# Logit steps of a differential attention, issued one by one or two at a time, in a two-layer fp32 encoder on one NeuronCore

## The chip, the core and the metric

The kernel runs on one core of a Trainium2 chip. A core has a matrix engine (PE, with its weight loads shown apart as PEld), a vector engine (DVE), a scalar engine for activations and scaled copies (ACT), a general-purpose engine (POOL), and a queue (SP) from which nearly all DMAs are issued here. Operands lie in an on-chip memory of 128 partitions; matrix products are written to a small accumulation memory (PSUM) of eight banks of 128 x 512 fp32, which DVE and ACT read. The engines run side by side and wait for each other on semaphores; each works through its own queue in order.

The metric is the time of one execution on the device in microseconds (us), the median of three runs.

## What is computed

Two layers over a sequence of 512 tokens of width 1024. Layer 0 mixes tokens by differential attention, layer 1 by a gated linear attention; each layer also attends to 256 memory tokens with four heads of 64, and is followed by a gated MLP with a short convolution. All is fp32. The change lies in layer 0:

```python
# differential attention: 6 heads, two maps of width 64 each, query blocks of 128
q = rms_norm(q, g0) * 64 ** -0.5;  k = rms_norm(k, g1)
logits = einsum('bhmqd,bhmkd->bhmqk', qb, k) + bias      # block-causal mask, chunks of 64
p = softmax(logits);  w = p[:, :, 0] - lam * p[:, :, 1]
o = rms_norm(einsum('bhqk,bhkv->bhqv', w, v), g) * (1 - lam_init)

# memory attention of the same layer
kv = rms_norm(mem, g) @ w_kv;  k, v = split(kv)
o_mem = softmax(rms_norm(q_mem) * 64 ** -0.5 @ rms_norm(k).T) @ v

x = x + concat([o, o_mem]) @ w_out
h = rms_norm(x);  u = conv(h @ w_up) + b;  a, g = split(u)
x = x + (silu(g) * a) @ w_down
```

## The kernel before

**The large products.** Every matrix product with weights is made in three passes: activations and weights are each split into a rounded part and a rest (`whi`/`wlo`, `xsh`/`xsl`; lines 253 and 256 for weights, 310 and 311 for activations), and high x high, high x low and low x high are added up in a bank (lines 330 to 332 for the input projections, 351 to 353 for the others). Weights arrive in blocks of up to 128 x 1024 in a ring of three `raw` tiles, ACT casts them and DVE subtracts.

**Filler.** In layer 0 the attention is written out as a script, `SCRIPT`, which `do` reads word by word. A number is a credit in us: `F.fill` takes that much from a queue of units of the large products (six products of 512 columns count 1.3, three count 0.65). A letter with a number is a step of the attention. So the script is the order in which PE gets its work; PE's queue is the only one in which the order is written by hand. DVE, ACT, POOL and SP get the order that the scheduler of the building layer makes of the same program.

**Steps.** Three pairs of heads (0/1, 2/3, 4/5) have five steps each, numbered 0 to 14 through all pairs: each step covers one or two query blocks with 512 or 384 + 128 or 256 + 256 key columns (`TOGETHER`), so that the logits of one map fill one bank. For step t:

- `Lt` (`logits`, line 719): products of 64 rows, the two maps on the two halves of the array, into two banks of tag `lg`; then for each map a minimum with the bias on DVE (`nmd`, line 726), an exponential on ACT (line 729), and on DVE the weights `p0 - lam * p1` (lines 734 to 738).
- `Mt`: the same with banks of tag `tp`. The entry exists in the table of letters, and the script before does not use it.
- `Tt` (`turn`): four transposes of the weights into a `tp` bank, copied out by ACT (line 748).
- `Vt` (`values`, line 760): products with v into the head's `sm` bank; behind a head's last one stands its normalisation (`output`, four squares on ACT, line 771).
- `Ph` (`prepare`): head h's q and k are turned by eight transposes into two `tp` banks, copied out by ACT (line 682). `Fh` turns the head's output into operands of the output projection; `sh` scales it.

The memory attention has its own letters. `a` and `b` split the memory tokens for the keys and values of layer 0 and 1 (four calls each, two row tiles at a time; `b3` is the last for layer 1, and the units of ("kv", 1) read it). `q0` normalises the memory queries, `q1` turns them by eight transposes through `tp` (line 582 copies out). `k0` and `k1` turn the keys of layer 0 and 1 through an `sm` bank, which ACT copies out (`kmT`, line 560). `l0` to `l3` are the logits of the four query blocks (line 591, 64 rows, `lg` banks), each with a maximum on DVE (line 599), four exponentials on ACT (line 603) and a scaling on DVE (line 607). `t0` to `t7` turn their weights (line 616), `v0` and `v1` make the products with the memory values (line 629) into an `sm` bank. `X` loads x for the residual, `O` starts the second part of the output projection, `N` normalises q or k of a pair.

**Banks.** PSUM's eight banks are four tags of two: `mm` for the large products, `sm`, `lg` and `tp`. A tile of a tag waits until the readers of the tile two back are done.

`MemAttn.logits` takes several blocks and gives the first one `lg` banks and the second `sm` in layer 1 and `tp` in layer 0; layer 1 calls it with two blocks, layer 0 with one.

Of the kernel before, what the change touches and what calls it, by code (L numbers as in the profile page):

```python
# [37 lines left out]

SCRIPT = """
    17.75 P0 3.9  # L40
    L0 a3 P1 8.45 a0 0.97
    L1 1.94 a1 T0
    L2 3.57 a2
    L3 T1 4.86 N2 V0 T2 N3 V1 12.33
    L4 P2 6.17 V2 T3
    L5 s0 T4 2.27 V3
    L6 P3 b1 V4 5.2 T5
    L7 T6 F0 7.14 b0
    L8 V5 T7 8.42 V6 s1 N5 N4 F1
    L9 V7 P4 b2 4.45 T8 T9 s2 3.0  # L50
    L10 V8 3.55 X P5 q0
    L11 b3 V9 T10 4.2
    L12 F2 V10 s3 T11 3.8 q1 k0
    L13 3.15 l0 V11 T12 3.65
    L14 F3 t0 3.3 V12 T13 t1 l1 3.9 T14 l2 t2 2.3 O k1 t3 s4 l3 v0 t4 V13 V14 t6 t5 1.3 t7 F4 v1 s5 F5 6.15 ! 4.55
"""

ORDER = (('v', 0), ('qk', 1), ('kv', 0), ('qk', 2), ('vm', 2), ('kv', 1))
# [28 lines left out]
def _pieces():  # L87

    plan = []

    def piece(key, name, i, ks, *ranges):
        plan.append((key, name, i, ks, ranges))

    for l in range(2):
        if l == 0:
            w = "w_in_diff"
            piece(("qk", 0), w, 0, K8, (0, 256), (768, 1024))
            for key in ORDER:
                if key[0] == "qk":
                    p = key[1]  # L100
                    piece(key, w, 0, K8, (256 * p, 256 * p + 256), (768 + 256 * p, 1024 + 256 * p))
                elif key[0] == "kv":
                    piece(key, "w_mem_kv", key[1], K8, (0, 512))
                elif key[0] == "vm":
                    p = key[1]
                    piece(key, w, 0, K8, (1536 + 256 * p, 1792 + 256 * p), (2304, 2560))
                else:
                    p = key[1]
                    piece(key, w, 0, K8, (1536 + 256 * p, 2048 + 256 * p))
        else:  # L110
            w = "w_in_gla"
            piece(("gm", 1), w, 0, K8, (2304, 2576))
            for c in range(5):
                piece(("g", c), w, 0, K8, (512 * c, min(512 * c + 512, 2304)))
        for i, part in enumerate(PASS[l]):
            for c, ks in part:
                piece(("o", l, i, c), "w_out", l, ks, (256 * c, 256 * c + 256))
        base = 0
        for nq in HALVES:
            for q in range(base, base + nq):  # L120
                piece(("ua", l, q), "w_up", l, K8, (256 * q, 256 * q + 256))
                piece(("ug", l, q), "w_up", l, K8, (DFF + 256 * q, DFF + 256 * q + 256))
            for c in range(4):
                piece(("dn", l, base, c), "w_down", l, tuple(range(2 * base, 2 * base + 2 * nq)),
                      (256 * c, 256 * c + 256))
            base += nq
    return plan


def _blocks():  # L130

    out = []
    for key, name, i, ks, ranges in _pieces():
        w = sum(b - a for a, b in ranges)
        step = WTILE // w
        out.append([(name, i, ks[j:j + step], ranges, w) for j in range(0, len(ks), step)])
    return out
# [42 lines left out]
def trunk(ctx, tc, head_d, x_t, mem_t, wpack, cols_a_d, cols_d, conv_d, gate_d, rel_bias, diff_lambda, consts, onehot, out):  # L180
# [12 lines left out]
    def bank(tag):  # L193
        return ps.tile([128, 512], F32, name=f"ps_{tag}", tag=tag)

    def xtile():
        return xs.tile([128, S], F32, name="xt", tag="xs", bufs=XS)
# [9 lines left out]
    def blk(b, w=128):  # L207
        return slice(w * b, w * b + w)
# [40 lines left out]
    plan, blocks, made = _pieces(), _blocks(), []  # L249
# [318 lines left out]
    class MemAttn:  # L568
# [13 lines left out]
                A.activation(self.qT[hp], p, AF.Copy, scale=c_mq(self.l))  # L582


        def logits(self, *blocks):
            banks = [(bank(tag), bank(tag)) for _, tag in zip(blocks, ("lg", "sm") if self.l else ("lg", "tp"))]
            for b, pl in zip(blocks, banks):
                for hp in range(2):
                    for j in range(2):
                        hh = blk(j, 64)  # L590
                        mm(pl[j][:, blk(hp, 256)], self.qT[hp][hh, blk(b)], kmT[self.l][hh, hp], start=True, stop=True)
            for b, pl in zip(blocks, banks):
                self.softmax(b, pl)
# [51 lines left out]
    def diff_layer(pool, mix, acc):  # L645
# [45 lines left out]
        def members(t):  # L691
            pr, s = divmod(t, len(TOGETHER))
            out, at = [], 0
            for j, i in TOGETHER[s]:
                out.append((2 * pr + j, i, 4 * j + i, at))
                at += 128 * (i + 1)
            return pr, out, at

        def bias(h):
            bt = heads[h]["bt"] = pool.tile([128, S], F32, name="bt", bufs=2)  # L700
            src = bass.AP(tensor=bias_d.tensor, offset=bias_d[h].offset + 1, ap=[[1, 128], [1, 512]])
            nc.sync.dma_start(bt, src)
            G.memset(bt[0:64, 0:64], -1e30)

        def logits(t, tag="lg"):
            pr, group, _ = members(t)
            P = pairs[pr]
            s2, nm, rc = P["s2"], P["nm"], P["rc"]
            for h, _, _, _ in group:
                if "bt" not in heads[h]:  # L710
                    bias(h)
            pls = bank(tag), bank(tag)
            for h, i, _, at in group:
                nk = 128 * (i + 1)
                cuts = (0, nk) if i == 0 else (0, nk // 2, nk)
                for k0, k1 in zip(cuts, cuts[1:]):
                    for m in range(2):
                        hh = blk(m, 64)
                        mm(pls[m][:, at + k0:at + k1], heads[h]["q"][hh, blk(i)], heads[h]["k"][hh, k0:k1],
                           start=True, stop=True)  # L720
            e = xtile(), xtile()
            for m in range(2):
                for h, i, g, at in group:
                    c = slice(at, at + 128 * (i + 1))
                    n1 = nm[:, 8 * m + g:8 * m + g + 1]
                    V.tensor_tensor_reduce(
                        out=e[m][:, c], in0=pls[m][:, c], in1=heads[h]["bt"][:, 127 + 128 * i::-1], scale=-1.0,
                        scalar=1e38, op0=ALU.add, op1=ALU.min, accum_out=n1)
                    A.activation(e[m][:, c], e[m][:, c], AF.Exp, scale=-1.0, bias=n1,
                                              accum_out=s2[:, m, g:g + 1])  # L730
            ids = sorted(g for _, _, g, _ in group)
            step = max(ids[-1] - ids[0], 1)
            b, lr = slice(ids[0], ids[-1] + 1, step), slice(8 + ids[0], 9 + ids[-1], step)
            V.reciprocal(rc[:, b], s2[:, 1, b])
            V.scalar_tensor_tensor(rc[:, lr], rc[:, b], nlam, s2[:, 0, b], op0=ALU.mult, op1=ALU.mult)
            for _, i, g, at in group:
                c = slice(at, at + 128 * (i + 1))
                V.scalar_tensor_tensor(e[1][:, c], e[1][:, c], rc[:, 8 + g:9 + g], e[0][:, c],
                                                    op0=ALU.mult, op1=ALU.add)
            live[t] = e[1]  # L740
# [57 lines left out]
        ma = MemAttn(pool, 0, qm, mix, False)  # L798
        ops, keys = [None] * 2, [None] * 2
        for key in ORDER:  # L800
# [16 lines left out]

        doing = {
            "L": logits, "M": lambda i: logits(i, "tp"), "T": turn, "V": values, "P": prepare, "F": finish,
            "N": lambda i: norms(i // 2, i % 2), "a": lambda i: ops[0]((2 * i, 2 * i + 1)),  # L820
            "b": lambda i: ops[1]((2 * i, 2 * i + 1)), "k": lambda i: keys[i]("sm"),
            "q": lambda i: ma.queries() if i else (F.need("v2"), ma.norm()),
            "l": lambda i: ma.logits(i), "t": ma.turn, "v": lambda i: ma.values(i, "sm"),
            "s": lambda i: scales.pop(i)(), "X": lambda i: load_x(x_t),
            "O": lambda i: last.append(out_proj(0, mix, 1, acc, 5)), "!": lambda i: F.flush()}
        do(SCRIPT, doing)
# [228 lines left out]
    def load_x(src):  # L1055
        for k in range(KT):
            xT[k] = xtile()
            nc.sync.dma_start(xT[k], src[k])
# [117 lines left out]
    for l in range(2):  # L1176
        with tc.tile_pool(name=f"at{l}", bufs=2) as pool:
            mix = [None] * 8
            sums, acc = acc, [None]
            if l == 0:  # L1180
                diff_layer(pool, mix, acc)
            else:
                gla_layer(pool, mix, sums)
                out_proj(1, mix, len(PASS[1]) - 1, acc)
                F.flush()
        with tc.tile_pool(name=f"ff{l}", bufs=2) as pool:
            acc = ffn(pool, l, acc)
# [73 lines left out]
```

## Time and profile before

| | |
|---|---|
| median of three runs | 1168.69 us (1168.32 to 1168.73) |
| the profiled execution | 1168.01 us |
| its span, first to last instruction | 1166.2 us |
| granted PE clock | 1.00 |
| DMA | 117.68 MB, 100 GB/s over the span |

Layer 0's attention with its output projection takes about the first 220 us of the span, then follow its MLP, layer 1's attention from about 600 us, and the second MLP. In the page, "Lnnn engine op out<-in" is a group of instructions by line, engine and tiles; "busy, mean" is its total time and the mean of one, and what stands behind the bar is idle time of that engine just ahead of them and what ended it. In the order of time each row has a start, a duration, the engine and the instructions merged in it. A product is recorded until its last result is written, so that neighbours overlap; the rate at which PE works is seen from one start to the next. An fp32 product that is no transpose takes two passes and has two records.

### The profile page before, as it was taken

What the parts mean: (1) busy time and instruction counts of PE and PEld (TensorE: products, weight loads), DVE (VectorE), ACT (ScalarE), POOL (GpSimd) and SP (SyncE); (2) the same over time, 40 slices, a digit from 0 to 9 for tenths busy, and PEclk for the clock granted to TensorE, in tenths of its full rate; (3) what the DMA queues carried; (4) which work ended last, traced back from release to release, by engine and by line L of the source; (5) the groups of instructions that cost most, each with busy time, mean ns of one, the idle gap of its engine ahead of it and who ended that gap; (6) DMA issues with size and microseconds to landing.
All of it is one profiled execution on the core that took longest, in us unless ns stands there. A gap on an engine that the chain in (4) does not pass through costs nothing.

```text
span 1166.2 us, 14790 instructions
## 1 busy us (share of the span) xinstructions
PE 1160.7 (100%) x5658; PEld 965.3 (83%) x5658; DVE 750.9 (64%) x1256; ACT 545.5 (47%) x951; POOL 5.0 (0%) x27
## 2 busy tenths in 40 slices
PE   9999999999999999999999999999999999999998
PEld 7888888888888888888888888988888888888887
DVE  7576778688677326677447637777876743576741
ACT  6676687555344213344437634436643421343420
POOL 0000000000000000000000000000000000000000
PEclk9999999999999999999999999999999999999999
DMA  8423242123223223222342230333232323232231
GB/s 295 158 70 99 78 141 73 63 103 130 85 90 120 83 88 124 75 91 98 120 148 68 81 108 3 110 121 109 93 123 73 98 102 108 85 114 73 89 101 45
DMA packets 39556, 117.68 MB, mean 101 GB/s; under 512 B 4703, under 2 KB 7192, under 8 KB 39486
## 3 DMA queue, kind: packets, MB, share of 16 engines
q1 hardware_dynamic: 39054, 116.35, 29.5%
q8 instruction: 44, 0.72, 0.3%
q10 hardware_dynamic: 432, 0.39, 0.1%
q14 instruction: 26, 0.21, 0.1%
HBM read 112.52 MB, written 4.21 MB: 100 GB/s over the span
## 4 chain that ended last, share of the span: by engine, by line
PE 98%; ACT 1%; DVE 1%; issue 0%; POOL 0%; DVEq 0%; POOLq 0%
PE ps_mm L352 9%; PE ps_mm L351 9%; PE ps_mm L353 9%; PE ps_sm L353 8%; PE ps_sm L352 8%; PE ps_sm L351 7%; PE ps_mm L330 6%; PE ps_mm L332 6%; PE ps_mm L331 6%; PE ps_tp L353 3%; PE ps_lg L353 3%; PE ps_lg L352 3%; PE ps_tp L352 3%; PE ps_lg L351 3%; PE ps_tp L351 3%; PE ps_tp L220 3%
## 5 line engine op out<-in xcount | busy, mean ns | idle before, releaser
L253 ACT CAST whi<-raw 128x1024 fp32r<-128x1024 f32 (+4 forms) x212 | 207.6, 986 | 245.4 <-PE ps_tp L352 120.9
L256 DVE TENSOR_TENSOR wlo<-raw,whi 128x1024 fp32r<-128x1024 f32 (+4 forms) x212 | 240.3, 1140 | 117.5 <-ACT whi L253 116.6
L351 PE MATMUL ps_mm<-xsh,whi 128*128 128x512 f32 x438 | 171.6, 392 | 0.0
L352 PE MATMUL ps_mm<-xsl,whi 128*128 128x512 f32 x438 | 170.6, 389 | 0.0
L353 PE MATMUL ps_mm<-xsh,wlo 128*128 128x512 f32 x438 | 170.5, 389 | 0.0
L351 PE MATMUL ps_sm<-xsh,whi 128*128 128x512 f32 x378 | 147.0, 389 | 0.0
L352 PE MATMUL ps_sm<-xsl,whi 128*128 128x512 f32 x378 | 147.0, 389 | 0.0
L353 PE MATMUL ps_sm<-xsh,wlo 128*128 128x512 f32 x378 | 147.0, 389 | 0.0
L330 PE MATMUL ps_mm<-whi,xsh 128*128 128x512 f32 (+2 forms) x336 | 129.1, 384 | 0.0
L332 PE MATMUL ps_mm<-whi,xsl 128*128 128x512 f32 (+2 forms) x336 | 126.1, 375 | 0.0
L331 PE MATMUL ps_mm<-wlo,xsh 128*128 128x512 f32 (+2 forms) x336 | 125.9, 375 | 0.0
L1113 ACT ACTIVATE cvo<-u,cv 128x512 f32<-128x512 f32 x88 | 71.4, 815 | 112.1 <-DVE u L1111 112.1
L352 PEld LDWEIGHTS ps_mm<-xsl,whi 128*128 128x128 f32 x438 | 82.3, 188 | 17.2 <-DVE xsl L311 0.4
L351 PEld LDWEIGHTS ps_mm<-xsh,whi 128*128 128x128 f32 x438 | 82.2, 188 | 17.1 <-issue 0.3
L353 PEld LDWEIGHTS ps_mm<-xsh,wlo 128*128 128x128 f32 x438 | 82.2, 188 | 17.1
L1114 DVE SCALAR_TENSOR_TENSOR cvo<-u,cv,cvo 128x512 f32<-128x512 f32 x88 | 65.7, 749 | 36.2 <-ACT cvo L1113 36.0
L352 PEld LDWEIGHTS ps_sm<-xsl,whi 128*128 128x128 f32 x378 | 70.9, 188 | 14.8
L351 PEld LDWEIGHTS ps_sm<-xsh,whi 128*128 128x128 f32 x378 | 70.9, 188 | 14.7
L353 PEld LDWEIGHTS ps_sm<-xsh,wlo 128*128 128x128 f32 x378 | 70.9, 188 | 14.7
L332 PEld LDWEIGHTS ps_mm<-whi,xsl 128*128 128x128 f32 x336 | 63.2, 188 | 11.6
L330 PEld LDWEIGHTS ps_mm<-whi,xsh 128*128 128x128 f32 x336 | 63.2, 188 | 11.3 <-ACT ks L659 0.3
L331 PEld LDWEIGHTS ps_mm<-wlo,xsh 128*128 128x128 f32 x336 | 63.3, 188 | 10.4
(295 smaller groups left out, 1760.1 us busy)
## 6 DMA issues: line engine op xcount, KB each, us to landing
raw<-in_wpack_dram SPq DMA_DIRECT2D x178, 512.0 KB, 3.5
xt<-in_x_t_dram SPq DMA_DIRECT2D x15, 256.0 KB, 5.2
raw<-in_wpack_dram SPq DMA_DIRECT2D x15, 256.0 KB, 3.0
raw<-in_wpack_dram SPq DMA_DIRECT2D x8, 384.0 KB, 3.0
xres<-xt SPq DMA_DIRECT2D x8, 256.0 KB, 3.0
xt<-xres SPq DMA_DIRECT2D x8, 256.0 KB, 5.4
out_dram<-xt SPq DMA_DIRECT2D x7, 256.0 KB, 2.0
bt<-bias_d SPq DMA_DIRECT2D x6, 256.0 KB, 4.1
```

What stands on the lines that cost most here:

```text
L220: nc.tensor.transpose(dst, src, ident[:n, :n])
L253: ins = A.copy(hi[:, c], raw[:, c])
L256: V.tensor_sub(lo[:, c], raw[:, c], hi[:, c].bitcast(F32))
L330: mm(p, sh[k][:, blk(b)], hi, start=k == 0, stop=False)
L331: mm(p, sh[k][:, blk(b)], lo, start=False, stop=False)
L332: mm(p, sl[k][:, blk(b)], hi, start=False, stop=k == KT - 1)
L351: mm(p, hi[:, blk(n)], bh, start=i == first, stop=False)
L352: mm(p, hi[:, blk(n)], bl, start=False, stop=False)
L353: mm(p, lo[:, blk(n)], bh, start=False, stop=i == last)
L1113: A.activation(c, u[:, 2:], AF.Identity, scale=cv[l][:, 2, j:j + 1], bias=cv[l][:, 3, j:j + 1])
L1114: V.scalar_tensor_tensor(c, u[:, 1:S + 1], cv[l][:, 1, j:j + 1], c, op0=ALU.mult, op1=ALU.add)
```

## The change

The script is written anew around the logit steps, one entry of the table of letters is extended and one added, and `MemAttn.logits` takes the tags from its caller if it gets them. With the steps of the new script: `L0 M1`, `L2 M3`, `L5 M6`, `L7 M8`, `L10 M11` and `L12 M13` stand next to each other, the first with `lg` and the second with `tp` banks; `L4` and `L9` stay alone; behind `L14` comes `m1`, the memory logits of the second block, on `tp` banks; `l2` now makes the memory logits of the third and the fourth block (`lg` and `tp`) and `l3` is gone. `T10` comes ahead of `P5`. `P` and `T` steps and fill credits between them have moved accordingly.

```diff
 SCRIPT = """
     17.75 P0 3.9
-    L0 a3 P1 8.45 a0 0.97
-    L1 1.94 a1 T0
-    L2 3.57 a2
-    L3 T1 4.86 N2 V0 T2 N3 V1 12.33
-    L4 P2 6.17 V2 T3
-    L5 s0 T4 2.27 V3
-    L6 P3 b1 V4 5.2 T5
-    L7 T6 F0 7.14 b0
-    L8 V5 T7 8.42 V6 s1 N5 N4 F1
+    L0 M1 a3 3.4 P1 5.05 a0 0.97
+    1.94 a1 T0
+    L2 M3 a2 3.57
+    T1 4.86 N2 V0 T2 N3 V1 12.33
+    L4 P2 3.9 P3 2.27 V2 T3 2.27 T4
+    L5 M6 s0 V3 b1 2.6 V4 1.3 T5 1.3
+    L7 M8 3.5 T6 F0 3.64 b0
+    V5 T7 8.42 V6 s1 N5 N4 F1
     L9 V7 P4 b2 4.45 T8 T9 s2 3.0
-    L10 V8 3.55 X P5 q0
-    L11 b3 V9 T10 4.2
-    L12 F2 V10 s3 T11 3.8 q1 k0
-    L13 3.15 l0 V11 T12 3.65
-    L14 F3 t0 3.3 V12 T13 t1 l1 3.9 T14 l2 t2 2.3 O k1 t3 s4 l3 v0 t4 V13 V14 t6 t5 1.3 t7 F4 v1 s5 F5 6.15 ! 4.55
+    L10 M11 V8 3.0 T10 2.9 X b3 V9 P5 q0 1.85
+    F2 V10 s3 T11 2.5
+    L12 M13 3.25 q1 k0
+    1.3 l0 V11 T12 3.65
+    L14 m1 3.9 F3 t0 V12 T13 0.65 t1 1.95 T14 t2 0.65 t3 1.3 l2 O 1.3 k1 s4 v0 t4 V13 V14 0.65 t6 t5 0.65 t7 F4 v1 s5 F5 6.15 ! 4.55
 """
...
-        def logits(self, *blocks):
-            banks = [(bank(tag), bank(tag)) for _, tag in zip(blocks, ("lg", "sm") if self.l else ("lg", "tp"))]
+        def logits(self, *blocks, tags=None):
+            banks = [(bank(tag), bank(tag)) for _, tag in zip(blocks, tags or (("lg", "sm") if self.l else ("lg", "tp")))]
...
-            "l": lambda i: ma.logits(i), "t": ma.turn, "v": lambda i: ma.values(i, "sm"),
+            "l": lambda i: ma.logits(*((2, 3) if i == 2 else (i,))), "m": lambda i: ma.logits(i, tags=("tp",)),
+            "t": ma.turn, "v": lambda i: ma.values(i, "sm"),
```

## The prediction

> **What bounds the kernel now.** I read the page's first part and its chain, then the windows by stage, then the order of time of PE, ACT and DVE around the steps that the script moves, and the groups of ACT and DVE with their shapes kept apart.
>
> ```profile
> span 1166.2 us, 14790 instructions
> PE 1160.7 (100%) x5658; PEld 965.3 (83%) x5658; DVE 750.9 (64%) x1256; ACT 545.5 (47%) x951; POOL 5.0 (0%) x27
> ...
> PE 98%; ACT 1%; DVE 1%; issue 0%; POOL 0%; DVEq 0%; POOLq 0%
> ```
>
> ```profile
> 180.00:220.00 40.00, 40.00 (x283) 32.74 (x283) 33.06 (x78) 25.65 (x85) 0.00 (x0) 1.00 0.14 47
> ```
>
> PE is busy for all but 5.5 us and carries 98% of the chain. So the change gains only what it takes out of PE's own queue, and time for which PE waits is added in full: nothing behind it has slack to give it back. The last row is one stage (after its 40 us come PE, PEld, DVE and ACT, then POOL, the clock and the DMAs): PE is full, but DVE has work for 33 us and ACT for 26. Here a few us of fresh work in front of something that PE needs come late.
>
> **What it takes out of PE.** A logit step runs on 64 rows of the array, two products side by side; all around it uses 128 rows. In the order of time on PE (start, duration, line), a step alone, a pair as the second attention already has it, and four transposes behind a step:
>
> ```profile
> 64.61 0.39 PE L332 MATMUL ps_mm<-whi,xsl 128*128 128x512 f32 x1
> 64.93 1.14 PE L719 MATMUL ps_lg<-kT,qT 64*128 64x256 f32 x8
> 65.99 0.50 PE L330 MATMUL ps_mm<-whi,xsh 128*128 128x512 f32 x1
> 66.33 0.40 PE L331 MATMUL ps_mm<-wlo,xsh 128*128 128x512 f32 x1
> ```
>
> ```profile
> 638.01 1.14 PE L591 MATMUL ps_lg<-kmT,xt 64*128 64x256 f32 x8
> 638.98 1.03 PE L591 MATMUL ps_sm<-kmT,xt 64*128 64x256 f32 x8
> 639.93 0.50 PE L330 MATMUL ps_mm<-whi,xsh 128*128 128x512 f32 x1
> ```
>
> ```profile
> 201.68 0.66 PE L220 MATMUL ps_tp<-C,xt 128*128 128x128 f32 x4
> 202.09 0.48 PE L351 MATMUL ps_mm<-xsh,whi 128*128 128x512 f32 x1
> ```
>
> ```profile
> 48.66 0.60 PE L220 MATMUL ps_tp<-C,ks 128*128 128x128 f32 x4
> 49.01 0.48 PE L330 MATMUL ps_mm<-whi,xsh 128*128 128x512 f32 x1
> 49.33 0.40 PE L331 MATMUL ps_mm<-wlo,xsh 128*128 128x512 f32 x1
> ```
>
> 512-column products otherwise follow each other after 0.23. Ahead of a lone step it is 0.32 (64.61 to 64.93), the step takes 1.06, and the product behind it 0.34: 0.09 + 1.06 + 0.11 = 1.26. A pair is 0.09 + 0.97 + 0.95 + 0.11 = 2.12, 0.40 under two alone. A bare step is then 0.97 + 0.95 - 1.06 = 0.86, and the switch costs 0.09 of draining and 0.11 of weight load on the way in, and as much on the way out. Where transposes stand behind a step it is 0.05 less: four of them take 0.41 there (201.68 to 202.09) and 0.35 elsewhere (48.66 to 49.01). Counted in the built order, the kernel has 21 such stretches, 19 of them in the first attention; the changed one has 13, and more of these end on the dearer side. 8 x 0.34 = 2.7.
>
> The transposes and values beside which the steps stood now stand alone between the large products: 47 stretches of small work become 57. A boundary more costs between nothing (0.35 + 0.32 in the last fence, for what takes 4 x 0.11 + 0.23) and 0.04; I take 0.02, together 0.2. So 2.5 comes off PE, bounds 2.2 and 3.1.
>
> The Trainium skill, TensorE: Matmul & The Clock Gate, Part 2, lets the queue pull weight loads ahead of running products. By it the two loads would be hidden already, only the two drains saved, and the term would be 8 x 0.18 = 1.4. The trace disagrees: a lone step is 0.11 longer than a pair's second one (1.06 against 0.95), which also ends in a switch.
>
> **What it adds: waits on PE.** Matmuls run in the order in which they are written, so one that waits holds all behind it. Number and kind of PE's instructions stay; so do the SP queue's loads, but that five loads of x go behind two loads of weights, and x is needed only by the output projection, long after; the bias loads and POOL's order are the same. What changes is who stands ahead of whom on ACT and DVE. Four places matter.
>
> A: the last memory operands (`b3`). They now come right ahead of `V9 P5 q0` and a fill whose first product reads them. In the built order of ACT the split stays behind head 5's two copies.
>
> ```profile
> 160.72 0.60 PE L220 MATMUL ps_tp<-C,qs 128*128 128x128 f32 x4
> 161.16 0.60 PE L220 MATMUL ps_tp<-C,ks 128*128 128x128 f32 x4
> ```
>
> ```profile
> 161.63 0.67 ACT L682 ACTIVATE qT<-ps_tp,cols 128x512 f32<-128x512 f32 x1
> 162.20 0.68 ACT L682 ACTIVATE kT<-ps_tp,cols 128x512 f32<-128x512 f32 x1
> ...
> 164.51 0.51 ACT L310 ACTIVATE xsh<-xt,cols_a 128x256 fp32r<-128x256 f32 x1
> ```
>
> From the first transpose: the first four end at 0.6, the copies step by 0.57 (161.63 to 162.20) to 1.75, the split ends at 2.3, and a product that waited loads its weights only then (0.1): 2.4. PE is there at 0.44 + 0.35 + 0.03 = 0.85. It waits 1.55 (bounds 1.2 and 1.7). Now `b3`'s first reader comes a turn and a fill later, which is the cover.
>
> B: the first memory logits (`l0`). The copy of the first keys on ACT falls behind the exponentials of two steps, and the fill ahead of `l0` is 1.3 instead of 3.15.
>
> ```profile
> 177.73 0.69 ACT L560 ACTIVATE kmT<-ps_sm,cols 128x512 f32<-128x512 f32 x1
> ```
>
> ```profile
> L253 ACT CAST whi<-raw 128x1024 fp32r<-128x1024 f32 x35 | 36.1, 1050 | 14.2 <-PE ps_mm L352 7.6 <-PE ps_mm L332 3.5 <-DMA raw<-in_wpack_dram 1.4
> ...
> L729 ACT ACTIVATE xt<-xt,nmd 128x384 f32<-128x384 f32 x12 | 7.3, 610 | 7.7 <-DVE nmd L726 7.7
> L729 ACT ACTIVATE xt<-xt,nmd 128x256 f32<-128x256 f32 x12 | 6.0, 498 | 2.7 <-DVE nmd L726 2.7
> ```
>
> Steps 12 and 13 have four exponentials of 256 columns, two of 384 and two of 128 (0.39, by the slope of the two rows): 4 x 0.5 + 2 x 0.61 + 2 x 0.39 = 4.0. Behind them ACT's built order has a cast of 1024 and one of 256 columns, two 256-wide evictions, a 512-wide square, the two query copies, a short logarithm, and then the keys: 0.95 + 0.3 + 2 x 0.4 + 0.5 + 2 x 0.57 + 0.1 + 0.69 = 4.5, each with the 0.1 off by which neighbours overlap (0.67 long, 0.57 apart). PE, from the pair's start: the pair and its exit 2.1, 15 products 3.4, twelve transposes 1.3, six products 1.4: 8.2. ACT, if DVE takes the first minimum at once (1.2 after the start, as in C's rows) and ends it 0.4 later: 1.6 + 4.0 + 4.5 = 10.1, a wait of 1.9. But DVE's built order has other work ahead of these minima:
>
> ```profile
> L256 DVE TENSOR_TENSOR wlo<-raw,whi 128x768 fp32r<-128x768 f32 x4 | 3.7, 954 | 0.0
> L390 DVE TENSOR_TENSOR qm<-qm,rs_y 128x1024 f32<-128x1024 f32 x1 | 1.2, 1225 | 0.0
> L726 DVE CUSTOM_DVE_ANT_0 xt<-ps_lg,bt 128x256 f32<-128x256 f32 x12 | 4.4, 420 | 1.3 <-PE ps_lg L719 1.3
> ```
>
> The memory queries' product, head 4's output (a 512-wide pass, 0.65 as in C) and two of the subtractions, 1.14 + 0.65 + 2 x 0.87 = 3.5, start about when the pair does. So the first minimum starts 2.4 later and ACT's chain ends at 12.5. The two `tp` banks that `q1` turns into are also held until step 13's minima have read them, at 3.6 + 4 x 0.33 + 0.7 = 5.6 and 0.8 later, and PE comes at 5.5: 0.8 of waiting there. PE then is at 9.0, and `l0` waits 3.5. Together 4.3; bounds 1.9 and 4.6. I take the upper part, since DVE is 83% busy here.
>
> C: the first memory values (`v0`). With `l2` and `l3` in one, eight exponentials stand on ACT ahead of the second layer's keys, and `v0` needs the `sm` bank in which these still are.
>
> ```profile
> 194.80 1.13 PE L591 MATMUL ps_lg<-kmT,xt 64*128 64x256 f32 x8
> ...
> 195.97 1.29 DVE L599 TENSOR_REDUCE nmm<-ps_lg 128x2 f32<-128x512 f32 x2 [0.67 <-PE ps_lg L591]
> ...
> 196.69 0.47 ACT L603 ACTIVATE xt<-ps_lg,nmm 128x256 f32<-128x256 f32 x1 [0.35 <-DVE nmm L599]
> ```
>
> From the pair's start: the first exponential after 1.9 (194.80 to 196.69), eight at 0.46 make 3.7, the keys 0.69: 6.3. PE: pair and exit 2.1, six products 1.4, four transposes 0.44: 3.9. It waits 2.4 (bounds 2.0 and 2.6).
>
> D: turns that need a `tp` bank, or a softmax, that is just then in DVE's queue. Each such wait is under one 512-wide pass (0.65). Nothing if all are covered, 2.0 if three are not at all; I take 1.3.
>
> Sum: 1.55 + 4.3 + 2.4 + 1.3 - 2.5 = +7.05. The profiled execution took 1168.0 (its span and 1.8 around it), 0.7 under the median. It becomes 1175.1, and the median of 1168.7 becomes 1175.7.
>
> **Rivals.** 1: cover is enough. ACT reaches the keys in time in B and C, as now, and only the 2.5 remains: 1166.2, faster. It decides once all waits together stay under 2.5, for which ACT's and DVE's chains would have to be 7 us shorter than their rows make them. 4%.
>
> 2: DVE isn't late in B, and D is covered: 1.55 + 1.9 + 2.4 - 2.5 = 3.4, so 1172.1. For it: what DVE has ahead is read from an order, not from a row. Against it its share of 83%. 16%.
>
> 3: a PE that stood still comes back slow.
>
> ```profile
> L446 PE MATMUL ps_tp<-idle 128*128 128x512 f32 x2 | 2.1, 1138 | 1.3 <-POOL idle L443 1.3
> ...
> L398 PE MATMUL ps_lg<-oh,rb 32*6 32x512 f32 x2 | 1.0, 588 | 0.0
> ```
>
> 512 columns cost 1138 ns in the first products of the run and 588 later, half the rate for some 3 us. The same again behind B's wait adds 1.5: 1177.2. Against it: the granted clock reads 1.00 in every stage, the first too. 8%. The Trainium skill, TensorE: Matmul & The Clock Gate, Part 1, has the clock halved after an idle window of about 3.4 us; no run here shows it.
>
> 4: a pair saves nothing, since its second step writes other banks (`tp`): +9.5, 1178.2. Row 638.98 speaks against it, a change of bank with no gap. 2%.
>
> **How the numbers follow.** 70% for the forecast, 30% for the four. The range goes halfway to rival 2 and takes in rival 3: 1173.2 to 1177.8. A measurement of this kernel tells about 0.2% (2.3 us) from no change: faster 0.04, same 0.05 (rival 2 with B and C at their lower bounds and less), slower 0.91.
>
> **What would show it.** On PE: `ps_lg` and `ps_tp` steps of 64 rows back to back, about 1.9 together, and 13 stretches instead of 21. Idle time of PE that is now nil: 3 to 4 us ahead of the first memory logits with ACT's copy of the keys as what ends it, 2 to 2.6 ahead of the memory values with the second keys, 1.5 at a product of the second memory projection with ACT's `xsh`, the rest with DVE; the busy time lower by about 2.5. It is wrong if these waits are missing, if they sum to less than 2.5, or if the time appears outside the first attention.

## The result and the profile after

| | before | after |
|---|---|---|
| median | 1168.71 us (1168.32 to 1169.2, 6 runs) | 1178.09 us (1176.38 to 1179.35, 6 runs) |
| the profiled execution | 1168.01 us | 1178.33 us |
| its span | 1166.2 us | 1176.5 us |
| granted PE clock, mean | 1.000 | 0.999 |

The ratio is 1.0082, with a 95% interval of 1.0071 to 1.0092: 9.4 us slower by the medians. The forecast was 1175.7 with a range up to 1177.8; the direction is right, the size 2.4 short (1.5 by a second set of runs, 1177.17, in the experiments).

The first rows of the page of the changed kernel, busy times and then the chain of waits:

```profile
span 1176.5 us, 14782 instructions
PE 1162.9 (99%) x5658; PEld 967.2 (82%) x5658; DVE 751.0 (64%) x1256; ACT 545.4 (46%) x951; POOL 5.0 (0%) x27
...
PE 94%; ACT 2%; DVE 2%; DMA 1%; issue 0%; SPq 0%; POOL 0%; DVEq 0%; ACTq 0%; POOLq 0%
```

PE now is idle for 13.6 us instead of 5.5, and ACT and DVE have a part in the chain. But its busy time has grown too, by 2.2 us, where fewer switches should have cut it. Both have to be explained. The view of PE's waits says where the idle time is (engine, tile and line, what it waited for; total, times, longest). Lines up to 821 are one less than before the change:

```profile
PE ps_lg L590 <- ACT kmT L559: 3.4, 1, 3.4
PE ps_sm L628 <- ACT kmT L559: 2.2, 1, 2.2
PE ps_mm L329 <- ACT xsh L309: 1.3, 1, 1.3
PE ps_tp L445 <- POOL idle L442: 1.3, 1, 1.3
PE ps_mm L329 <- ACT qm L849: 0.6, 1, 0.6
```

Three of these are new and stand where the prediction put them: B ahead of the first memory logits (L590), C ahead of the memory values (L628), A at a product of the second memory projection (L329). The wait of 1.3 for `idle` is at the start of both kernels. The last row, 0.6 in layer 1, was in nobody's list.

The busy time is explained by the order of time on PE behind B (start, duration, instructions merged):

```profile
182.66 0.40 PE L352 MATMUL ps_mm<-xsh,wlo 128*128 128x512 f32 x1
186.49 1.14 PE L590 MATMUL ps_lg<-kmT,xt 64*128 64x256 f32 x8 [3.43 <-ACT kmT L559]
187.55 1.76 PE L759 MATMUL ps_sm<-v,xt 128*128 128x128 f32 x8
189.11 1.06 PE L219 MATMUL ps_tp<-C,xt 128*128 128x128 f32 x4
189.82 0.78 PE L350 MATMUL ps_mm<-xsh,whi 128*128 128x512 f32 x1
190.39 0.63 PE L351 MATMUL ps_mm<-xsl,whi 128*128 128x512 f32 x1
190.82 0.63 PE L352 MATMUL ps_mm<-xsh,wlo 128*128 128x512 f32 x1
191.25 0.44 PE L350 MATMUL ps_mm<-xsh,whi 128*128 128x512 f32 x1
191.53 0.40 PE L351 MATMUL ps_mm<-xsl,whi 128*128 128x512 f32 x1
```

Large products start 0.43 apart (190.39, 190.82, 191.25) instead of 0.23, and are recorded with 0.63 instead of 0.40. That ends at 191.5. It doesn't begin with the work: the first memory logits still take 1.06 from start to start (186.49 to 187.55), as without a wait; the products behind them are slow. The windows name the cause (after the width come PE, PEld, DVE, ACT and POOL, then the granted clock):

```profile
180.00:184.00 4.00, 2.89 (x18) 2.07 (x16) 3.37 (x14) 4.00 (x14) 0.00 (x0) 1.00 0.15 55
184.00:188.00 4.00, 1.51 (x11) 1.14 (x12) 3.56 (x10) 2.53 (x6) 0.00 (x0) 0.99 0.45 164
188.00:192.00 4.00, 4.00 (x18) 3.57 (x17) 2.77 (x6) 2.41 (x9) 0.00 (x0) 0.58 0.00 0
192.00:196.00 4.00, 4.00 (x26) 2.96 (x24) 2.60 (x5) 1.05 (x1) 0.00 (x0) 1.00 0.01 1
```

Four us at a clock of 0.58 lose 4 x 0.42 = 1.7 us. The row that the prediction showed for 180 to 220 us read 1.00; it now reads 0.96. In the page's line of 40 slices this does not show, and in the mean it is the 0.999: 1.7 us are 0.0015 of the span. That is most of the 2.2. The rest, and the saving that should have lowered the busy time, are made up by waits of which a part is recorded as busy (A is 1.56 by the starts of the products and 1.31 in the view of waits) and by a start of the run that was 0.7 longer in this profile.

### The profile page after: what moved, and what is told of

Same layout as the page of the kernel before. It is cut to its first block, busy times and chain, and to the rows that moved or that the text cites. A ratio compares the mean times of both kernels' runs of the same rounds, so it can differ in the third digit from the quotient of the medians.

```text
span 1176.5 us, 14782 instructions
## 1 busy us (share of the span) xinstructions
PE 1162.9 (99%) x5658; PEld 967.2 (82%) x5658; DVE 751.0 (64%) x1256; ACT 545.4 (46%) x951; POOL 5.0 (0%) x27
## 4 chain that ended last, share of the span: by engine, by line
PE 94%; ACT 2%; DVE 2%; DMA 1%; issue 0%; SPq 0%; POOL 0%; DVEq 0%; ACTq 0%; POOLq 0%
PE ps_mm L351 8%; PE ps_mm L350 8%; PE ps_mm L352 8%; PE ps_sm L351 7%; PE ps_sm L350 7%; PE ps_sm L352 7%; PE ps_mm L329 6%; PE ps_mm L331 6%; PE ps_mm L330 6%; PE ps_lg L351 3%; PE ps_lg L352 3%; PE ps_lg L350 3%; PE ps_tp L351 3%; PE ps_tp L350 3%; PE ps_tp L352 3%; PE ps_tp L219 2%
## 5 line engine op out<-in xcount | busy, mean ns | idle before, releaser
L329 PE MATMUL ps_mm<-whi,xsh 128*128 128x512 f32 (+2 forms) x336 | 129.8, 386 | 1.9 <-ACT xsh L309 1.3
L329 PEld LDWEIGHTS ps_mm<-whi,xsh 128*128 128x128 f32 x336 | 63.2, 188 | 13.6 <-ACT xsh L309 1.6
```

The lines of the kernel that those rows point to most:

```text
L329: mm(p, sh[k][:, blk(b)], hi, start=k == 0, stop=False)
```

## The experiments

Each kernel was timed against the kernel before on the same chip; "over before" is the difference of those two medians. The median of before was 1168.47 to 1168.75 in these sets, with single runs from 1167.5 to 1170.5.

| kernel | median us | ratio, 95% interval | granted clock of the runs |
|---|---|---|---|
| keys first (k1 ahead of l2) | 1175.01 | 1.0056, 1.0043 to 1.0070 | 0.997 to 0.999 |
| b3 early | 1174.97 | 1.0053, 1.0040 to 1.0066 | 0.998 to 1.000 |
| late steps single | 1171.53 | 1.0030, 1.0018 to 1.0042 | 0.997 to 1.000 |
| memory single | 1174.87 | 1.0052, 1.0038 to 1.0066 | 0.997 to 0.999 |
| early pairs only | 1167.79 | 0.9993, 0.9984 to 1.0002 | 1.000 |
| six pairs | 1166.90 | 0.9985, 0.9976 to 0.9994 | 1.000, one 0.999 |
| changed again | 1177.17 | 1.0077, 1.0064 to 1.0089 | 0.997 to 0.999 |

**C: the second layer's keys first.** From the changed kernel:

```diff
-... t3 1.3 l2 O 1.3 k1 s4 v0 ...
+... t3 1.3 k1 l2 O 1.3 s4 v0 ...
```

> The changed kernel with k1 ahead of l2, so that ACT copies the second layer's memory keys before the eight exponentials. If C is a wait for that copy, it goes as a whole: no idle time of PE ahead of the memory values (L628), 9.4 - 2.3 = 7.1 over the kernel before, about 1175.8. Rival: the wait only moves to the next that needs those exponentials (a turn, or the values themselves), and the time stays at about 1178. The 3.5 us ahead of the first memory logits and the half rate behind them stay in both.

Measured: 6.5 over before. The wait ahead of L628 is gone from the view of waits, the 3.4 ahead of L590 is not, and nothing took C's place. So C was the copy behind eight exponentials. The 7.1 expected was 0.6 too high, within the spread of these runs (1174.2 to 1176.9). Against the changed kernel's two medians, 9.4 and 8.6 over before, the gain is 2.1 to 2.9; C is 2.3 long.

**A, and B in pieces: b3 early.** From the changed kernel:

```diff
-    L10 M11 V8 3.0 T10 2.9 X b3 V9 P5 q0 1.85
+    L10 M11 V8 3.0 b3 T10 2.9 X V9 P5 q0 1.85
```

> The changed kernel with b3 ahead of T10. A goes, and what was B's 3.5 us comes in three pieces, at the two banks for q1 (about 1.8 and 0.8) and at l0 (1.7). Theory: the products behind l0 ran at half rate because PE had stood still for 3.5 us in one piece; with pieces under 2 us the half rate is gone too, and the time is 9.4 - 1.6 (A) - 1.6 (rate) = 6.2 over before, 1174.9. Rival: the half rate belongs to that place (the idle time in sum, or what runs there) and stays: 7.8 over before, 1176.5.

Measured: 6.4 over before, near the theory's 6.2, but not for its reason alone, as its windows will show. Its view of waits:

```profile
PE ps_sm L628 <- ACT kmT L559: 2.3, 1, 2.3
PE ps_tp L219 <- DVE nmd L725: 1.7, 1, 1.7
PE ps_lg L590 <- ACT kmT L559: 1.6, 1, 1.6
```

and its windows, behind the two pieces of B and around C:

```profile
180.00:200.00 20.00, 18.19 (x110) 14.28 (x108) 18.00 (x44) 14.05 (x46) 0.00 (x0) 1.00 0.19 55
210.00:214.00 4.00, 2.07 (x26) 2.07 (x28) 2.16 (x6) 1.88 (x7) 0.00 (x0) 0.84 0.00 0
214.00:218.00 4.00, 4.00 (x32) 3.63 (x29) 1.45 (x3) 0.85 (x3) 0.00 (x0) 0.73 0.00 0
```

A is gone, and two waits of 1.7 and 1.6 within 7 us leave the clock at 1.00 where one of 3.4 halved it. In sum they are as long, so in this profile the sum is not what counts. But here the clock falls behind C, 4 x 0.16 + 4 x 0.27 = 1.7 us that the theory did not have: C's 2.3 did nothing to the clock in the changed kernel's profile, so a standstill of that length can do it, and need not. The two runs at a clock of 1.000 are 4.5 and 5.7 over before, under the theory's 6.2; that the median came out near it is partly luck.

**The late steps one by one.** The lines of steps 10 to 13 as before the change; early pairs and paired memory logits stay.

```diff
-    L10 M11 V8 3.0 T10 2.9 X b3 V9 P5 q0 1.85
-    F2 V10 s3 T11 2.5
-    L12 M13 3.25 q1 k0
-    1.3 l0 V11 T12 3.65
+    L10 V8 3.55 X P5 q0
+    L11 b3 V9 T10 4.2
+    L12 F2 V10 s3 T11 3.8 q1 k0
+    L13 3.15 l0 V11 T12 3.65
```

> The changed kernel with the lines of steps 10 to 13 as they were before; the pairs up to step 8 and the paired memory logits stay. Theory: A, B, the half rate and the wait of a turn (D) near them go; C stays with 2.3 and 1.1 of small waits with DVE; five pairs save some 1.7 and the step behind L14 some 0.3. 2.2 over before, 1170.9. Rival: pairs save nothing; then about 4 over before, 1172.8. If the 0.7 by which the median of the changed kernel is over waits, rate and saving belongs to the early pairs (the start of the run, or layer 1's load of the gate weights), it is 1171.6.

Measured: 3.0 over before, 0.8 above the theory's 2.2 and at the number of the third possibility. A and B are gone from its view of waits and C is there with 2.3. Its six runs go from 1170.32 at a clock of 1.000 to 1174.7 at 0.997: the lower the clock, the longer the run. So the 0.8 is most likely half rate behind C, the one long wait that is left, in some executions and not in others. Only the run at 1.000 has a profile, so where the clock fell in the others is not shown. Against a longer start of the run: the two kernels below that have the early pairs and no C lack the 0.8.

**The memory logits one by one.** The line of step 14 as before, and `l2` for one block; the pairs up to L12 M13 stay.

```diff
-    L14 m1 3.9 F3 t0 V12 T13 0.65 t1 1.95 T14 t2 0.65 t3 1.3 l2 O 1.3 k1 s4 v0 ...
+    L14 F3 t0 3.3 V12 T13 t1 l1 3.9 T14 l2 t2 2.3 O k1 t3 s4 l3 v0 ...
...
-            "l": lambda i: ma.logits(*((2, 3) if i == 2 else (i,))),
+            "l": lambda i: ma.logits(i),
```

> The changed kernel with the line of step 14 as before (memory logits one by one, k1 where it was); the pairs up to L12 M13 stay. Theory: C goes (2.3) and two pairs' saving (0.5) with it, A and B stay with 1.6 + 4.1, and the half rate behind B; six pairs save 1.5: 4.2 + 1.6 to 2.8 over before, 1174.4 to 1175.6. Rival: C's wait is hidden in what B delays, and the time stays at 1177.

Measured: 6.1 over before, within the range. C is not hidden behind B: without it the time is lower.

**The early pairs alone.** The diffs of the last two kernels together, so that the script is the old one from step 10 on:

```diff
     L7 M8 3.5 T6 F0 3.64 b0
     V5 T7 8.42 V6 s1 N5 N4 F1
     L9 V7 P4 b2 4.45 T8 T9 s2 3.0
-    L10 M11 V8 3.0 T10 2.9 X b3 V9 P5 q0 1.85
+    L10 V8 3.55 X P5 q0
...
```

> Only the pairs up to step 8 (L0 M1, L2 M3, L5 M6, L7 M8) of the changed kernel; all from step 9 on and the memory logits as before. Theory: no wait of more than 0.2, four pairs at 0.34 save about 1.3: 1.0 to 1.3 under before, 1167.6. Rival: a pair saves nothing and its moved neighbours cost: 0.4 over before, 1169.1.

Measured: 0.75 under before, the interval just reaching no change. Beside the one at the start, PE has no wait over 0.5. By the median a pair saves 0.19, less than the 0.34 that was reckoned with; that a pair saves anything is clear of noise only with six, below.

**Is it the standstill?** To the kernel before, with no pair in it, n copies were added on ACT ahead of the copy of the first memory keys; nothing reads what they write:

```diff
+            if l == 0:
+                ex = xtile()
+                for _ in range(10):
+                    A.copy(ex, p)
             A.activation(kmT[l].rearrange("p a b -> p (a b)"), p, AF.Copy, scale=c_mk(l))
```

> The kernel before, unpaired, with ten more copies of the same 512-wide tile on ACT ahead of its copy of the first memory keys (their result is read by nothing). PE then stands still for about 2.2 us ahead of the first memory logits, with nothing else changed. Theory: a standstill halves PE's rate afterwards by its length alone, and 2.2 us already do it in some executions, as behind C in the kernel with b3 early: 2.3 to 4 over before, the clock of the runs between 0.998 and 1.000. Rival: only a standstill of 3.4 us and more counts: 2.3 over before in every run, clock 1.000. Second rival: the half rate belongs to the paired steps: 2.3 over before too.

> The same with fourteen copies: PE stands still for 4.5 us. Both theories of a standstill: behind it half rate for some 3.4 us, 4.5 + 1.7 = 6.2 over before, 1174.8, clock 0.999 or less in every run. Rival that the half rate belongs to the paired steps of the changed kernel and not to the standstill: 4.5 over before, 1173.1, clock 1.000.

Both copies and their neighbours on ACT cost more than reckoned: the view of waits has 5.0 and 7.9, not 2.2 and 4.5, so the first of the two said nothing yet about a short standstill. Then with six, eight and seven:

> The kernel before with six more copies on ACT ahead of its copy of the first memory keys. Ten copies made PE wait 4.9 us and fourteen 7.8, 0.73 a copy, so six make 1.9 to 2.0. Theory, from the standstills seen so far (2.3 us did it in some executions, pieces under 1.9 did not): at most a few of the runs show a lower clock, 2.0 to 2.8 over before, 1170.9. Rival: half rate behind every standstill, however short: 2.0 + 1.5 and more, over 1172. Second rival: up to 3.4 us nothing: 2.0 over before, clock 1.000 in all.

> The same with eight copies: PE waits 3.4 us, as B does in the changed kernel. Theory: the half rate follows in every run and costs 1.5 to 2.8; 4.9 to 6.2 over before, 1174, clock 0.997 to 0.999. Rival that the length of the standstill sets how long the rate is halved: 3.4 + 1.7 with 3.4 us of half rate, and ten and fourteen copies would have had more than the 2.8 and 2.7 that they showed beyond their waits.

> The kernel before with seven more copies on ACT ahead of its copy of the first memory keys. Six made PE wait 1.7 us and eight 3.4 (start to start), so seven make some 2.5, about C's length in the changed kernel. Six cost their wait alone (1.7 over before), eight 1.7 beyond it. Theory: at 2.5 us it depends on the execution; 2.5 plus 0 to 2.5 over before, about 1172.0, with clocks from 0.997 to 1.000 among the runs. Rival: a sharp bound near 3.4 us: 2.5 over before, 1171.2, clock 1.000 in all.

The standstill here is the time from the start of the last product to that of l0 in the order of time, less the 0.32 that this takes with no wait:

| copies | standstill us | over before | more than the standstill | clock of the runs |
|---|---|---|---|---|
| 6 | 1.7 | 1.7 | 0.0 | 1.000, two of eleven 0.999 |
| 7 | 2.6 | 2.8 | 0.2 | five of seven 1.000, then 0.999 and 0.997 |
| 8 | 3.4 | 5.1 | 1.7 | 0.997 to 0.999 |
| 10 | 5.1 | 7.7 | 2.6 | 0.997 to 0.999 |
| 14 | 8.0 | 10.5 | 2.5 | 0.996 to 0.997 |

PE behind six copies, and behind fourteen:

```profile
183.83 1.20 PE L595 MATMUL ps_lg<-kmT,xt 64*128 64x256 f32 x8 [1.64 <-ACT kmT L564]
184.96 1.16 PE L764 MATMUL ps_sm<-v,xt 128*128 128x128 f32 x8
```

```profile
190.38 2.15 PE L595 MATMUL ps_lg<-kmT,xt 64*128 64x256 f32 x8 [7.91 <-ACT kmT L564]
192.45 2.07 PE L764 MATMUL ps_sm<-v,xt 128*128 128x128 f32 x8
```

The same eight products take 1.16 and 2.07. (With the copies, lines behind line 560 are four more than in before.) With eight copies, the granted clock accounts for all of the surplus: 4 x 0.26 + 4 x 0.16 = 1.7.

```profile
184.00:188.00 4.00, 3.17 (x17) 2.83 (x18) 2.57 (x8) 3.16 (x10) 0.00 (x0) 0.74 0.40 131
188.00:192.00 4.00, 4.00 (x19) 3.40 (x18) 3.17 (x9) 2.76 (x8) 0.00 (x0) 0.84 0.02 4
```

The same windows of keys first, whose standstill ahead of l0 is 3.4 too:

```profile
184.00:188.00 4.00, 2.31 (x9) 1.49 (x10) 2.83 (x9) 1.73 (x5) 0.00 (x0) 0.67 0.52 164
188.00:192.00 4.00, 4.00 (x16) 3.71 (x16) 2.80 (x6) 2.52 (x9) 0.00 (x0) 0.50 0.00 0
192.00:196.00 4.00, 4.00 (x24) 3.08 (x25) 2.00 (x3) 1.05 (x1) 0.00 (x0) 0.98 0.00 0
```

Here the clock loses 4 x 0.33 + 4 x 0.50 + 4 x 0.02 = 3.4, twice as much. At a clock of 0.50 that is 6.8 us of half rate, against 3.4 us with eight copies, in the changed kernel (both profiles), in b3 early and in memory single. Ten copies have 6.8 in their profile and fourteen 10.2. So in these eight profiles the half rate lasts 3.4 us or a multiple of it, and the same standstill can bring one or two of these. What of it falls within the standstill costs nothing: with fourteen copies 5.6 of the 10.2.

No pair is needed for the half rate, so the rival that it belongs to the paired steps falls. At 1.7 us it stays away: of the two runs at 0.999 one is the profiled one, and all its windows of 5 us read 1.00 (a run of before reads 0.999 too, so that figure alone proves nothing). At 2.6 most runs have none, while two of the seven, at 0.999 and 0.997, are 4.5 and 6.0 over before; from 3.4 on no run reads 1.000. The medians of the surplus, 1.7, 2.6 and 2.5, can't be told apart with five runs each: by the intervals they are 0.5 to 3.4, 1.0 to 4.0 and 0.5 to 3.8. No growth with the standstill is seen.

**The changed kernel once more**, unchanged, beside these.

> The changed kernel once more, for a second profile beside these kernels. The waits A, B and C have fixed lengths (1.6, 0.6 + 3.5, 2.3) whatever the execution; the half rate behind them has not, so the runs spread over some 3 us and the lower the clock of a run the longer it is. If the 0.7 at the start of the run and the 1.0 at layer 1's gate weights belong to the change, they stand in this profile too; if they are scatter of the loads, they don't.

Measured: 1177.17, 8.6 over before. The waits are those of the first profile to 0.1. The 0.7 at the start is not there, and starts of the run (to the first turn of head 0's queries) differ by 1.2 us among the profiles whatever the kernel, so that part was scatter. The wait in layer 1 is there, with 0.4.

**Six pairs without the waits.** From the changed kernel: `b3` goes ahead of 2.3 of filler, of `P5` and of `V9`, `L12`, `L13` and `l1` stand alone, `k1` stands ahead of the paired `l2`.

```diff
-    L10 M11 V8 3.0 T10 2.9 X b3 V9 P5 q0 1.85
-    F2 V10 s3 T11 2.5
-    L12 M13 3.25 q1 k0
-    1.3 l0 V11 T12 3.65
-    L14 m1 3.9 F3 t0 V12 T13 0.65 t1 1.95 T14 t2 0.65 t3 1.3 l2 O 1.3 k1 s4 v0 t4 V13 V14 0.65 t6 t5 0.65 t7 F4 v1 s5 F5 6.15 ! 4.55
+    L10 M11 V8 2.6 b3 2.3 X P5 q0
+    V9 T10 2.85
+    L12 F2 V10 s3 T11 3.8 q1 k0
+    L13 3.15 l0 V11 T12 3.65
+    L14 F3 t0 3.3 V12 T13 t1 l1 3.9 T14 t2 1.3 t3 k1 l2 1.0 O s4 v0 t4 V13 V14 t6 t5 1.3 t7 F4 v1 s5 F5 6.15 ! 4.55
```

> The changed kernel with the pairs up to L10 M11 and the paired memory logits of the last two blocks, but b3 two fills ahead of its reader, L12 and L13 alone, l1 by itself, and k1 ahead of the paired l2. Theory: without A, B and C six pairs at 0.2 to 0.34 remain, 1.2 to 1.7 under before: 1167.1. Rival: what pairs save is eaten by small waits with DVE: not under 1168.2.

Measured: 1166.90, 1.6 under before, as the theory had it, and the only kernel whose interval is below 1. Its page, and its view of PE's waits in full:

```profile
span 1164.8 us, 14789 instructions
PE 1159.2 (100%) x5658; PEld 965.7 (83%) x5658; DVE 750.3 (64%) x1256; ACT 545.0 (47%) x951; POOL 5.0 (0%) x27
```

```profile
PE ps_tp L445 <- POOL idle L442: 1.3, 1, 1.3
PE ps_lg L909 <- DVE xsh L899: 0.5, 1, 0.5
PE ps_lg L976 <- DVE xt L970: 0.2, 1, 0.2
PE ps_tp L219 <- DVE xt L964: 0.2, 1, 0.2
```

These four were in the kernel before as well. PE's busy time is 1.5 lower, and nothing was added.

## Why the prediction was right in kind and too low

**What bounds the kernel:** right. PE was full, and what it waited for was added; the kernel with six pairs shows that what is saved on it is gained.

**The saving on PE:** right for the pairs themselves, too high for what a kernel gains by them. From the early pairs, a pair between large products, and then the second step of another pair, behind four transposes:

```profile
53.56 1.14 PE L718 MATMUL ps_lg<-kT,qT 64*128 64x192 f32 x12
54.54 1.03 PE L718 MATMUL ps_tp<-kT,qT 64*128 64x256 f32 x8
55.50 0.50 PE L329 MATMUL ps_mm<-whi,xsh 128*128 128x512 f32 x1
```

```profile
110.51 1.22 PE L718 MATMUL ps_tp<-kT,qT 64*128 64x256 f32 x8
111.65 1.16 PE L759 MATMUL ps_sm<-vv,xt 128*128 128x128 f32 x8
```

The first pair takes 0.98 + 0.96, against 0.97 + 0.95 in the prediction, and four transposes left alone (75.50 there) take 0.45, against 4 x 0.11. PE's weight loads show the switch itself: in before, the load for the large product at 64.61 starts at 64.39, while that of the lone step starts with it, at 64.93. But the second step at 110.51 takes 1.14: it writes the two `tp` banks, and ACT copies the transposes ahead of it out of one of these until 110.54. At 125.77, four transposes take 0.59 instead of 0.43. These two, 0.3 together, are waits of D's kind that no view names, and both are in the changed kernel too. Set against the eight lone steps of before, four pairs save 1.3 (0.32 each, against 0.34 reckoned); less the 0.3 that is 1.0, and the median has 0.75; six gave 1.64. Net that is 0.19 to 0.27 a pair: the switch was priced rightly, and small waits take a part of it back. Rival 4, that a pair saves nothing, falls.

**A:** right. In the order of time (PE, then ACT, of the changed kernel) the product starts 1.92 after the second four transposes do, where 0.36 would be free of waiting: 1.56 against 1.55 forecast. ACT has the two copies of head 5 and then the split, in the order that was read off the built program:

```profile
166.00 0.60 PE L219 MATMUL ps_tp<-C,ks 128*128 128x128 f32 x4
167.92 0.50 PE L329 MATMUL ps_mm<-whi,xsh 128*128 128x512 f32 x1 [1.31 <-ACT xsh L309]
```

```profile
166.21 0.69 ACT L681 ACTIVATE qT<-ps_tp,cols 128x512 f32<-128x512 f32 x1 [2.71 <-PE ps_tp L219]
166.79 0.68 ACT L681 ACTIVATE kT<-ps_tp,cols 128x512 f32<-128x512 f32 x1
167.36 0.90 ACT L309 ACTIVATE xsh<-xt,cols_a 128x256 fp32r<-128x256 f32 x2
```

**B:** right, and so was the upper choice within its bounds. The pair starts at 174.07; DVE has the queries' product, head 4's output and two subtractions first:

```profile
173.84 1.23 DVE L389 TENSOR_TENSOR qm<-qm,rs_y 128x1024 f32<-128x1024 f32 x1
...
175.17 0.69 DVE L778 TENSOR_TENSOR o<-ps_sm,rs 128x512 f32<-128x512 f32 x1
175.78 1.82 DVE L255 TENSOR_TENSOR wlo<-raw,whi 128x768 fp32r<-128x768 f32 x2
177.51 0.42 DVE L725 CUSTOM_DVE_ANT_0 xt<-ps_lg,bt 128x256 f32<-128x256 f32 x1
```

```profile
174.07 1.16 PE L718 MATMUL ps_lg<-kT,qT 64*128 64x128 f32 x16
```

```profile
177.97 0.51 ACT L728 ACTIVATE xt<-xt,nmd 128x256 f32<-128x256 f32 x1 [2.96 <-DVE nmd L725]
...
185.74 0.69 ACT L559 ACTIVATE kmT<-ps_sm,cols 128x512 f32<-128x512 f32 x1
```

The first minimum starts 3.4 after the pair (1.2 + 2.4 forecast), and ACT ends the keys at 186.43, 12.4 after it (12.5). l0 starts 3.83 behind the last product, 3.5 more than with no wait, which was the forecast; at q1's banks it was 0.6 instead of 0.8. Rival 2, that DVE isn't late, falls with the row at 177.51: ACT waited 2.96 for it.

**C:** right. 2.3 against 2.4, for the named reason; keys first shows it. **D:** some 1.0 by the distances of starts, the two above among them, against 1.3 taken. With these, A, B (4.1) and C are 9.0; less the 2.5 for eight pairs that is 6.5, where the forecast had +7.05. From the first turn of head 0 to the same large product behind the attention PE takes some 8.7 longer than before; without 1.7 of half rate that is 7.0. Either way the sum that was made holds, to about half a us.

**The step that failed** is the one that kept rival 3 apart: "Against it: the granted clock reads 1.00 in every stage, the first too. 8%." A clock that reads 1.00 in a kernel that never stands still says nothing of one that does, and the forecast itself put 3.5 us of standstill in one place. The reason against it was drawn from the wrong kernel; the only rows that bore on it, 1138 ns and 588 for 512 columns at the start, spoke for it. Nor did the first stage speak against it: its windows from 2 to 4 us read 1.00 beside those very products at 1138, so either the reading misses a slow start or they were slow for another reason, which stays open. The runs showed in its place a clock of 0.50 for 3.4 us, or twice that, behind B: 1.7 us or up to 3.4. Had the half rate been in the sum, it would have said 1177.2; the two medians are 1178.09 and 1177.17. The price of 1.5 was near the first profile's 1.7; keys first, profiled at a clock of 0.997, pays nearly twice that.

The Trainium skill, TensorE: Matmul & The Clock Gate, Part 1, was right that the clock halves behind an idle window of about 3.4 us, and that its phase varies from run to run. Here no run with a standstill of 3.4 us or more in one piece reads 1.000. But by their clocks and times 2.6 us did it in two runs of seven, and 2.3 us did it in the profile of b3 early, so a standstill below 3.4 is not yet safe.

**Outside the first attention** the prediction allowed nothing. In layer 1 PE waited 0.6 and 0.4 for a product of the queries on ACT, behind the load of the gate weights. Some delayed kernels show it (b3 early) and others don't (keys first). Whether it comes from the delay or is scatter of that load stays open; with the spread of the half rate it is what separates 1177.2 from 1178.1.

## What to carry to other kernels

Where one engine is full, a saving in its queue of 0.2 us a pair of steps is real, but every step that is made larger puts its followers' work in one lump on the other engines; before pairing, count what then stands ahead of the next operand in their queues. In a kernel like this, price a standstill of PE at its length up to 1.7 us, and at 1.7 or up to 3.4 more from 3.4 us on; between these it depends on the execution. In the one profile that has them, two waits of 1.7 and 1.6 left the clock alone where one of 3.4 halved it, so a wait that can't be removed may be worth splitting.

## What was not expected of the hardware

The half rate follows a standstill of 2.6 us in two runs of seven, and in none of the profiles with 1.7. It lasts 3.4 us or a multiple of it (6.8 in two profiles, 10.2 in one), so the same wait costs 1.7 us in one execution and up to 3.4 in another. It need not begin when PE stops or starts: in the changed kernel PE is back at work at 186.49, and by the windows and the rows the clock falls about 1.5 us later. And a granted clock of 0.999 over the whole span, which looks like nothing, stood for 1.7 us here, most of the 2.4 that the prediction missed.
